# Two-matmul products for 256-token layers: joined activation parts in one 512-column stream, 256-column weight groups, feed-forward in quarters

## The chip, the cores and the metric

The kernel runs on one NeuronCore of a Trainium2 chip, as one program launched once. The metric is the device time of one execution in microseconds (us); lower is better. Three executions of the kernel before are known, and one more execution was profiled. The core's engines are named as the profile names them: PE (TensorE), with PEld for its weight loads, DVE (VectorE), ACT (ScalarE), POOL (GpSimd) and SP (SyncE, which here only starts transfers).

## The reference

The reference is a network in float32 on 256 tokens of width 2048, with 256 context tokens and 256 memory tokens. Two layers of a first block come first (projection `w_in`, attention with pooling and Fourier branches, gate, projection `w_out`; the context tokens go through layer 0 whole and give only keys and values in layer 1). Then a second block: an even layer (sparse attention and a recurrent mixer, `even_w_out`), an odd layer (a state-space mixer with `odd_w_in`, `s5_w_glu` and `odd_w_out`), and after each of the two an attention on the memory (`xattn_wq`, `xattn_wo`) and a feed-forward layer:

```python
h = rms_norm(x, g)                       # x: 256 tokens of 2048 channels
x = x + square(relu(h @ ffn_up)) @ ffn_down   # 2048 -> 8192 -> 2048
```

Nearly all of the arithmetic is products of a [256 or 512, K] activation with a weight matrix. They must keep float32 accuracy, which the kernel reaches by splitting both operands in two parts.

## The kernel before, in words

**Products.** Activations are held transposed, channels on partitions and tokens along the free axis. `split` (L306) cuts a float32 tensor into an upper part `hi`, a cast to `float32r` on ACT (L308), and a lower part `lo`, the rest, on DVE (L309). `weights` (L317) brings a weight tile of two 128-row blocks by 512 columns (512 KB) from HBM through `raw` (L311) into a buffer `wraw`, a DMA that SP starts (L314), and splits it into `wh` and `wl`. The activations lie in tiles `hl[:, k]` of shape [128, 2, 256]: for channel block k the upper part `xh` and, right behind it, the lower part `xl`.

`mm_t` (L336) makes out^T = W^T x. For every channel block k and every output tile j of 128 columns of W it issues three matmuls into the same 256 columns of a PSUM bank, `wh` by `xh` (L344), `wh` by `xl` (L345) and `wl` by `xh` (L346); below, such a k and j are called a pair. Each matmul has its own load of 128 by 128 weights. Two output tiles share a bank [128, 2, 256]. `mm_n` (L348) is the form with tokens on the output's partitions, with the weights as the 512-column stream.

`dense_t` (L354) walks over W in groups of 512 columns; each group takes two PSUM banks of the four that bear the name `acc`, runs over all channel blocks, and hands each bank to an `evac` function. It yields after every weight tile. Work in the background (generators in `self.bg`) is advanced by `tick` (L239) at a rate per yield. `dense_norm` (L476) is `dense_t` on an activation that is scaled and split at its first use (`scaled`, L464, and `scale_split`, L452, L455 on ACT and L456 on DVE). `add_evac` (L485) adds a bank to the residual stream with one DVE instruction of 128x512 (L491) and, where asked, adds squares to the next norm's sums (`stat_add`, L414 and L419).

**Buffers.** In the second block `wraw` has three buffers (`WR2`), `wh` and `wl` two (`WB2`) and, inside `wide`, a third. In the first block all have three.

**Feed-forward.** `ffn` (L1611) works in eight parts of 1024 hidden channels: `up(q)` fills a tile `hid` of eight blocks (two buffers of it), `down(q)` adds its product to the stream. The order is up 0, up 1, down 0, up 2, down 1, and so on. The evacuation of `up` squares the rectified values and splits them (L1626 to L1629, per bank). During the feed-forward of the even layer, `s5_gen` runs in the background; it prepares the odd layer's matrices, mostly on DVE.

**Order of the instructions.** Each engine has its own stream. The framework orders instructions within it by a simulated timeline and by the priority that follows from program order (`schedule_with_timeline_sim=True`); there is no order written out by hand for the products.

**Where products of 256 tokens are.** In layer 1 of the first block the gates (L876, columns 2560 on of `w_in`) and `w_out` (L920); in the even layer `rkv_gen` for one half of the heads (L1132), and `even_w_out` in two halves; `xattn_wq` and `xattn_wo`, twice each; `ffn_up` and `ffn_down`, twice each; `odd_w_in`, `s5_w_glu` and `odd_w_out`. Layer 0 of the first block has 512 tokens, so its `mm_t` streams 512 columns per matmul.

Of the kernel before, what the change touches and what calls it, by code (L numbers as in the profile page):

```python
# [14 lines left out]
ALU = mybir.AluOpType  # L15
# [31 lines left out]
# ---------------------------------------------------------------- host layouts  # L47
# [28 lines left out]
# channels of the state space layer: (32 groups) (4 of their 8 x 4: last) (8: first) (16 in a group)  # L76
# [35 lines left out]
# ---------------------------------------------------------------- constants of the shapes  # L112
# [29 lines left out]
def _make_consts1():  # L142
    # axial rope of 256 positions in rows of 64
# [44 lines left out]
def _pool_consts():  # L188
    """[n', group, n]: pooled[n] = sum over n' of u[n'] times this."""
# [11 lines left out]
def _dft_consts():  # L201
    cn, sn = _dft(256)
    a = np.stack([cn, sn], 1).astype(np.float32)  # [n', 2, n]
# [3 lines left out]
def _dftc_consts():  # L207
    cc, sc = _dft(128)
    nrm = 1.0 / np.sqrt(256.0 * 128.0)
    return np.stack([cc * nrm, -sc * nrm], 1).astype(np.float32)  # [c', 2, c]  # L210


# ---------------------------------------------------------------- the program
class Prog:
# [17 lines left out]
    def wide(self, name):  # L232
        """a third buffer for the parts of weights."""
# [4 lines left out]
    # ---- work in the background: generators that are advanced between steps of the foreground  # L238
# [62 lines left out]
    def held(self, op):  # L301
        """keeps an instruction behind those that its engine was given before, where that is asked for."""
# [14 lines left out]
    def weights(self, W, r0, nk, c0, ncols):  # L317
        """nk*128 rows of W from r0, ncols columns from c0, as an exact sum of two parts."""
        nc = self.nc
        w = self.raw(W, r0, nk, c0, ncols)  # L320
        self.turn = (self.turn + 1) % 3
        p, n = (self.wx, 1) if self.wx and self.turn == 0 else (self.wp, self.wbuf)
        wh = p.tile([128, KB, 512], F32R, name="wh", bufs=n)
        wl = p.tile([128, KB, 512], F32R, name="wl", bufs=n)
# [3 lines left out]
    def weights_in(self, p, tag, W, r0, c0):  # L328
        """the same for KB * 128 rows and 512 columns in memory of p."""
# [24 lines left out]
    def dense_t(self, W, r0, nk, c0, ncols, X, ntok, evac, mt=128, cstep=512):  # L354
        """out^T = W^T x: X(k) gives (hi, lo) as [128, ntok]; evac(first tile, bank [128, n, ntok])."""
        per = 512 // ntok
        for cb in range(0, ncols, cstep):
# [3 lines left out]
            for k0 in range(0, nk, KB):  # L361
                n = min(KB, nk - k0)
                wh, wl = self.weights(W, r0 + k0 * 128, n, c0 + cb, cw)
                for kk in range(n):
                    k = k0 + kk
                    xh, xl = X(k)
                    self.mm_t(accs, per, wh, wl, kk, cw, mt, xh, xl, k == 0, k == nk - 1)
# [8 lines left out]

    def dense_n(self, W, r0, nk, c0, ncols, X, tbs, evac, bank=None, pre=()):
        """out = x W in natural layout: X(k) gives (hi, lo) as [128, tokens]; evac(col offset, tb, bank [128, cols]).
        pre: memory (pool, tag) for the first steps' weights."""
        pre = list(pre)  # L380
        for cb in range(0, ncols, 512):
            cw = min(512, ncols - cb)
            accs = {tb: (bank or self.acc)() for tb in tbs}
            for k0 in range(0, nk, KB):
                n = min(KB, nk - k0)
                wh, wl = self.weights_in(*pre.pop(0), W, r0 + k0 * 128, c0 + cb) if pre else self.weights(W, r0 + k0 * 128, n, c0 + cb, cw)
                for kk in range(n):
                    k = k0 + kk
                    xh, xl = X(k)
                    for tb in tbs:  # L390
                        s = slice(tb * 128, tb * 128 + 128)
                        self.mm_n(accs[tb][:, :cw], wh, wl, kk, cw, xh[:, s], xl[:, s], k == 0, k == nk - 1)
# [28 lines left out]
    def stat_cols(self, st, out, pair):  # L421
        """PSUM columns out [128, 2 or 4]: the sums of every token block."""
# [10 lines left out]
    def bcast(self, cols, n):  # L433
        """columns [128 tokens, n] of token blocks as rows on all partitions: PSUM [128, n*128]."""
# [6 lines left out]
    def rstd_bc(self, st, eps, pair=True):  # L441
        """1/sqrt(mean square + eps) of every token, on all partitions, as a PSUM bank."""
# [9 lines left out]
    def scale_split(self, hl, src, g, p):  # L452
        """split of src [128, 256] times a column."""
# [4 lines left out]
    def rstd_tile(self, st, eps, p):  # L458
        """rstd_bc of a pair in SBUF."""
# [4 lines left out]
    def scaled(self, x, g, p):  # L464
        """X(k) of x * g, made at the first use."""
# [3 lines left out]
        def X(k):  # L469
# [3 lines left out]
            return hl[:, k, 0], hl[:, k, 1]  # L473
        return X

    def dense_norm(self, W, ncols, x, st, g, p, evac, rate=0.0):  # L476
        """out^T = W^T (x * g) for x [128, 16, 256], in columns of 512; evac(first tile, bank, 1/rms tile)."""
        X = self.scaled(x, g, p)
        r = []
        gen = self.dense_t(W, 0, KT, 0, ncols, X, T, lambda j, ps: evac(j, ps, r[0]))  # L480
# [1667 lines left out]
```

## Time and profile before

| | |
|---|---|
| three executions | 3907.92, 3908.26, 3910.87 us; median 3908.26 |
| the profiled execution, span | 3909.9 us |
| its instructions | 66146 |
| PE busy | 3725.4 us, 26960 matmuls |
| DVE busy | 2584.0 us |
| ACT busy | 1626.1 us |
| DMA | 701.46 MB, 179 GB/s on the mean |

The profiled execution's own time is known as its span, 3909.9 us from the first to the last instruction; it lies between the lowest and the highest of the three executions and 1.6 us above their median. PE is busy in nine tenths or more of nearly every fortieth of the span. A matmul's row in the profile covers its whole passage through the engine, and several are under way at once, so that the duration of one matmul (283 ns) is longer than the time from one start to the next. What a matmul costs is read from the distance of the starts. The granted clock of PE (PEclk) is 1.00 when it runs at 2.4 GHz and 0.5 at 1.2 GHz.

### The profile page before, as it was taken

Reading aid. Unit: us, or ns where it says so; the run is one execution under the profiler, and the core shown is the slowest. Engines: PE = TensorE matmul, PEld = TensorE weight load, DVE = VectorE, ACT = ScalarE, POOL = GpSimd, SP = SyncE. Lnnn points to the kernel's source line nnn. Section 1 sums busy time; section 2 is a strip of 40 time slices with the busy share of each in tenths; the row PEclk is TensorE's granted clock in tenths of the full one; section 3 lists DMA queues with packets and bytes.
Section 4 is the critical chain, followed back from the end, with each engine's and each line's share of the span. In section 5 each row is a group of like instructions: output and inputs, shape, how many; then the busy total and the mean of one; then the engine's idle time right before and its main releaser. Section 6 shows DMA issues by size and latency. Waiting matters only on the chain.

```text
span 3909.9 us, 66146 instructions
## 1 busy us (share of the span) xinstructions
PE 3725.4 (95%) x26960; PEld 3373.3 (86%) x26960; DVE 2584.0 (66%) x4288; ACT 1626.1 (42%) x2334; POOL 101.7 (3%) x138
## 2 busy tenths in 40 slices
PE   6999999999999999899999999999789999999998
PEld 2677777777899899788999999998679999999997
DVE  3578787666766878667967866675555665555555
ACT  3323233252454556335444433443334454444443
POOL 0010000001000001000000000000000000000000
PEclk8999999999999999999999999999889999999999
DMA  9645444555644434524656765668995455555554
GB/s 338 242 147 177 156 156 162 176 170 183 211 151 157 135 118 145 158 82 142 199 185 191 225 189 182 197 210 237 212 195 183 151 173 184 184 183 183 184 183 142
DMA packets 418913, 701.46 MB, mean 179 GB/s; under 512 B 52208, under 2 KB 112752, under 8 KB 415280
## 3 DMA queue, kind: packets, MB, share of 16 engines
q1 hardware_dynamic: 385840, 662.39, 55.0%
q10 hardware_dynamic: 31488, 30.64, 2.4%
q8 instruction: 211, 3.46, 0.4%
q0 software_dynamic: 1280, 4.20, 0.3%
q14 instruction: 94, 0.77, 0.1%
HBM read 672.63 MB, written 24.51 MB: 178 GB/s over the span
## 4 chain that ended last, share of the span: by engine, by line
PE 84%; DMA 8%; DVE 5%; ACT 2%; issue 1%; SPq 1%; ACTq 0%; POOL 0%; DVEq 0%; POOLq 0%
PE acc L344 21%; PE acc L346 21%; PE acc L345 21%; PE acc L350 3%; PE acc L352 3%; PE acc L351 3%; DMA wraw<-ada_w 2%; DVE wl L309 1%; PE sm L588 1%; DMA tts<-KD 1%; PE sm L565 1%; ACT wh L308 1%; DMA wraw<-w_in 1%; DMA xc<-xc 1%; PE sm L539 1%
## 5 line engine op out<-in xcount | busy, mean ns | idle before, releaser
L309 DVE TENSOR_TENSOR wl<-wraw,wh 128x1024 fp32r<-128x1024 f32 x994 | 1207.7, 1216 | 838.8 <-ACT wh L308 831.0
L308 ACT CAST wh<-wraw 128x1024 fp32r<-128x1024 f32 x994 | 1036.4, 1044 | 1663.4 <-PE acc L345 1241.8
L344 PE MATMUL acc<-hl,wh 128*128 128x256 f32 (+1 forms) x3696 | 1111.4, 303 | 17.4 <-ACT hl L455 7.3
L345 PE MATMUL acc<-hl,wh 128*128 128x256 f32 (+1 forms) x3696 | 1106.5, 301 | 3.1 <-DVE hl L456 3.1
L346 PE MATMUL acc<-hl,wl 128*128 128x256 f32 (+2 forms) x3696 | 1090.7, 301 | 4.8 <-DVE wl L309 4.8
L344 PEld LDWEIGHTS acc<-hl,wh 128*128 128x128 f32 x3696 | 704.7, 191 | 56.9 <-issue 15.7
L345 PEld LDWEIGHTS acc<-hl,wh 128*128 128x128 f32 x3696 | 706.2, 191 | 33.9 <-issue 10.3
L346 PEld LDWEIGHTS acc<-hl,wl 128*128 128x128 f32 (+1 forms) x3696 | 699.9, 192 | 38.4 <-issue 10.1
L344 PE MATMUL acc<-hid,wh 128*128 128x256 f32 x2048 | 577.6, 283 | 1.2 <-ACT wh L308 1.2
L345 PE MATMUL acc<-hid,wh 128*128 128x256 f32 x2048 | 577.1, 283 | 0.0
L346 PE MATMUL acc<-hid,wl 128*128 128x256 f32 x2048 | 574.5, 283 | 0.0
L344 PEld LDWEIGHTS acc<-hid,wh 128*128 128x128 f32 x2048 | 388.8, 190 | 1.8 <-ACT wh L308 1.4
L346 PEld LDWEIGHTS acc<-hid,wl 128*128 128x128 f32 x2048 | 387.9, 190 | 2.8 <-issue 2.6
L345 PEld LDWEIGHTS acc<-hid,wh 128*128 128x128 f32 x2048 | 389.4, 190 | 0.2 <-issue 0.2
L536 DVE SCALAR_TENSOR_TENSOR ada_a<-wraw,sc,ada_a 128x512 f32<-128x512 f32 x360 | 252.5, 745 | 17.2 <-DMA wraw<-ada_w 16.9
L350 PE MATMUL acc<-wh,hl 128*128 128x512 f32 (+1 forms) x504 | 200.0, 402 | 1.5 <-ACT hn_q L606 1.5
L351 PE MATMUL acc<-wh,hl 128*128 128x512 f32 (+1 forms) x504 | 199.8, 396 | 0.0
L352 PE MATMUL acc<-wl,hl 128*128 128x512 f32 (+1 forms) x504 | 188.6, 394 | 3.3 <-DVE wl L309 3.3
L350 PEld LDWEIGHTS acc<-wh,hl 128*128 128x128 f32 x504 | 96.6, 192 | 28.9 <-issue 4.0
L352 PEld LDWEIGHTS acc<-wl,hl 128*128 128x128 f32 x504 | 94.8, 190 | 27.8 <-DVE wl L309 5.6
L491 DVE TENSOR_TENSOR xc<-acc,xc 128x512 f32<-128x512 f32 x160 | 108.7, 689 | 9.9 <-PE acc L346 8.2
L351 PEld LDWEIGHTS acc<-wh,hl 128*128 128x128 f32 x504 | 96.3, 191 | 20.6 <-issue 2.0
(591 smaller groups left out, 4935.2 us busy)
## 6 DMA issues: line engine op xcount, KB each, us to landing
wraw<-ffn_up SPq DMA_DIRECT2D x256, 512.0 KB, 3.7
wraw<-ffn_down SPq DMA_DIRECT2D x256, 512.0 KB, 3.8
wraw<-ada_w SPq DMA_DIRECT2D x192, 512.0 KB, 4.5
wraw<-w_in SPq DMA_DIRECT2D x144, 512.0 KB, 4.4
wraw<-w_out SPq DMA_DIRECT2D x64, 512.0 KB, 4.7
wraw<-even_w_in SPq DMA_DIRECT2D x54, 512.0 KB, 3.6
wraw<-even_w_out SPq DMA_DIRECT2D x32, 512.0 KB, 3.6
wraw<-xattn_wkv SPq DMA_DIRECT2D x32, 512.0 KB, 4.7
```

The costliest lines, as they stand in the source:

```text
L308: nc.scalar.copy(hi, src)
L309: self.held(nc.vector.tensor_tensor(lo, src, hi.bitcast(F32), op=ALU.subtract))
L344: nc.tensor.matmul(A, h, xh, start=(start and first), stop=False)
L345: nc.tensor.matmul(A, h, xl, start=False, stop=False)
L346: nc.tensor.matmul(A, lo, xh, start=False, stop=(stop and last))
L350: nc.tensor.matmul(A, xh, wh[:, kk, :cw], start=start, stop=False)
L351: nc.tensor.matmul(A, xl, wh[:, kk, :cw], start=False, stop=False)
L352: nc.tensor.matmul(A, xh, wl[:, kk, :cw], start=False, stop=stop)
L491: nc.vector.tensor_tensor(x[:, j:j + n], ps, x[:, j:j + n], op=ALU.add)
L536: nc.vector.scalar_tensor_tensor(a[:, r], w[:, kk], c, a[:, r], op0=ALU.mult, op1=ALU.add)
L539: nc.tensor.matmul(acc[32 * cb:32 * cb + 32], self.cst("pick")[:, r], a[:, r], start=r == 0, stop=r == nr - 1)
L565: nc.tensor.matmul(S[:, off:off + w], qT[:, qb * 128:qb * 128 + 128], kT, start=i == 0, stop=i == len(kTs) - 1)
```

## The change

A new function `dense_p` takes the place of `dense_t` wherever the product has 256 tokens, but for the low-rank products of the recurrent mixer (`lora_gen`), the first half of `s5_w_glu` (`glu_gen`), `memkv` and `rkv_stream`, which stay as they were. Per pair it issues two matmuls: `wh` by the activation tile [128, 2, 256] as one stream of 512 columns into a whole PSUM bank, and `wl` by `xh` into the second half of that bank. The first half of the bank then holds `wh xh`, the second `wh xl + wl xh`, and the evacuation adds the halves.

A weight tile is now four 128-row blocks by 256 columns (also 512 KB, with rows of 1 KB instead of 2 KB in HBM). A group is 256 columns wide and takes two banks, one for each output tile. `add_evac`, the new `out_evac_p` of layer 1 and the odd layer's `out_evac` add each half of each bank to the stream with its own DVE instruction. All other evacuations go through `joined`: a copy of one half by ACT and an addition by DVE for each bank, into an SBUF tile [128, 2, 256], which the old evacuation then reads.

The feed-forward works in four parts of 2048 hidden channels with one `hid` tile of sixteen blocks: up 0, down 0, up 1, down 1, and so on. Comments and docstrings are dropped throughout, and `X(k)` returns the joined tile. The core of the diff:

```diff
-    def raw(self, W, r0, nk, c0, ncols, tag="wraw"):
+    def raw(self, W, r0, nk, c0, ncols, tag="wraw", kb=KB):
...
-        w = p.tile([128, KB, 512], F32, name="wraw", tag=tag, bufs=bufs)
+        w = p.tile([128, kb, KB * 512 // kb], F32, name="wraw", tag=tag, bufs=bufs)
...
+    def dense_p(self, W, r0, nk, c0, ncols, X, evac):
+        nc = self.nc
+        kb = 2 * KB
+        for cb in range(0, ncols, 256):
+            accs = [self.acc((2, T)) for _ in range(2)]
+            for k0 in range(0, nk, kb):
+                wh, wl = self.weights(W, r0 + k0 * 128, kb, c0 + cb, 256, kb)
+                for kk in range(kb):
+                    k = k0 + kk
+                    xp = X(k)
+                    for j, A in enumerate(accs):
+                        cs = slice(128 * j, 128 * j + 128)
+                        nc.tensor.matmul(A, wh[:, kk, cs], xp, start=k == 0, stop=False)
+                        nc.tensor.matmul(A[:, 1], wl[:, kk, cs], xp[:, 0], start=False, stop=k == nk - 1)
+                    if kk == 1 and self.sub:
+                        self.tick(self.sub)
+                if k0 + kb < nk:
+                    yield
+            evac(cb // 128, accs)
+            yield
+
+    def joined(self, f, p, bufs=1):
+        def evac(j, accs):
+            s = p.tile([128, 2, T], F32, name="joined", bufs=bufs)
+            for i, A in enumerate(accs):
+                self.nc.scalar.copy(s[:, i], A[:, 1])
+                self.nc.vector.tensor_tensor(s[:, i], A[:, 0], s[:, i], op=ALU.add)
+            f(j, s)
+        return evac
...
-        def f(j, ps):
-            n = ps.shape[1]
-            nc.vector.tensor_tensor(x[:, j:j + n], ps, x[:, j:j + n], op=ALU.add)
+        def f(j, accs):
+            for h in range(2):
+                for i, A in enumerate(accs):
+                    nc.vector.tensor_tensor(x[:, j + i], A[:, h], x[:, j + i], op=ALU.add)
...
-                        yield from self.dense_t(W, 0, KT, 2560 + c0, 512, Xt, nt, gate_evac(c0))
+                        if last:
+                            yield from self.dense_p(W, 0, KT, 2560 + c0, 512, Xt, self.joined(gate_evac(c0), p))
+                        else:
+                            yield from self.dense_t(W, 0, KT, 2560 + c0, 512, Xt, nt, gate_evac(c0))
...
-                    n = 15 - turns(gt, K1)
+                    n = (11 if last and g else 15) - turns(gt, K1)
...
-        HT, NQ = 8, 8
+        HT, NQ = 16, 4
...
-            def up(q):
-                hid[q] = p.tile([128, HT, 2, T], F32R, name="hid", bufs=2)
+            for q in range(NQ):
+                hid = p.tile([128, HT, 2, T], F32R, name="hid")
...
-                gen = self.dense_t(a["ffn_up_2"][l], 0, KT, q * HT * 128, HT * 128, X, T, evac)
+                gen = self.dense_p(a["ffn_up_2"][l], 0, KT, q * HT * 128, HT * 128, X, self.joined(evac, p))
...
-            up(0)
-            for q in range(1, NQ):
-                up(q)
-                down(q - 1)
-            down(NQ - 1)
+                self.run(self.dense_p(a["ffn_down_2"][l], q * HT * 128, HT, 0, D, lambda k: hid[:, k], self.add_evac(x, st_out if q == NQ - 1 else None)), rate)
```

## Rows read from the trace of the kernel before

**Rows 1.** The page: busy time of PE, then the shares of the last chain.

```profile
PE 3725.4 (95%) x26960; PEld 3373.3 (86%) x26960; DVE 2584.0 (66%) x4288; ACT 1626.1 (42%) x2334; POOL 101.7 (3%) x138
...
PE 84%; DMA 8%; DVE 5%; ACT 2%; issue 1%; SPq 1%; ACTq 0%; POOL 0%; DVEq 0%; POOLq 0%
```

**Rows 2.** Windows: busy us (count) of each engine, PEclk, DMA share, GB/s.

```profile
1500.00:1600.00 100.00, 96.02 (x837) 90.96 (x836) 85.16 (x174) 56.47 (x112) 12.41 (x18) 1.00 0.49 156
1838.00:1862.00 24.00, 21.75 (x169) 21.34 (x168) 21.72 (x56) 14.73 (x26) 3.06 (x3) 0.93 0.51 160
2640.00:2700.00 60.00, 55.07 (x455) 52.06 (x455) 34.61 (x58) 22.83 (x31) 0.87 (x1) 0.94 0.81 239
3200.00:3800.00 600.00, 600.00 (x5002) 600.00 (x5002) 338.63 (x343) 250.24 (x266) 0.00 (x0) 1.00 0.59 183
```

**Rows 3.** Timeline of the second feed-forward layer: start us, us, matmuls 48 apart.

```profile
3400.21 0.28 PE L344 MATMUL acc<-hl,wh 128*128 128x256 f32 x1
...
3405.97 0.28 PE L344 MATMUL acc<-hl,wh 128*128 128x256 f32 x1
```

**Rows 4.** Timeline of PE in layer 0's `w_out`: matmuls 51 apart.

```profile
640.05 0.39 PE L344 MATMUL acc<-hl,wh 128*128 128x512 f32 x1
...
651.61 0.39 PE L344 MATMUL acc<-hl,wh 128*128 128x512 f32 x1
```

**Rows 5.** Groups by line and form: the first of every pair's three matmuls.

```profile
L344 PE MATMUL acc<-hl,wh 128*128 128x256 f32 x3168 | 902.4, 287 | 11.7 <-ACT hl L455 7.3 <-ACT wh L308 4.1 <-DVE rope_t L691 0.2
L344 PE MATMUL acc<-hid,wh 128*128 128x256 f32 x2048 | 577.6, 283 | 1.2 <-ACT wh L308 1.2
...
L344 PE MATMUL acc<-mx,wh 128*128 128x256 f32 x256 | 72.4, 286 | 3.4 <-ACT mx L308 3.4
...
L344 PE MATMUL acc<-yh,wh 128*128 128x256 f32 x256 | 71.1, 283 | 0.0
...
L344 PE MATMUL acc<-yb,wh 128*128 128x256 f32 x128 | 36.4, 294 | 0.0
L344 PE MATMUL acc<-ya,wh 128*128 128x256 f32 x128 | 36.0, 286 | 0.1
...
L344 PE MATMUL acc<-xol,wh 128*128 128x256 f32 x128 | 33.7, 287 | 0.0
```

**Rows 6.** Groups by line and form: the split of a weight tile.

```profile
L309 DVE TENSOR_TENSOR wl<-wraw,wh 128x1024 fp32r<-128x1024 f32 x976 | 1192.4, 1223 | 829.0 <-ACT wh L308 821.5 <-PE acc L346 3.5 <-PE sm L751 1.6
L308 ACT CAST wh<-wraw 128x1024 fp32r<-128x1024 f32 x976 | 1022.9, 1049 | 1644.8 <-PE acc L345 1233.8 <-PE acc L351 130.0 <-DMA wraw<-w_in 47.4
```

**Rows 7.** Waits from 3200 to 3800: us in total, times, longest.

```profile
ACT wh L308 <- PE acc L345: 326.6, 195, 1.8
```

**Rows 8.** DMA: weight loads issued from 3200 to 3800, 512 KB each.

```profile
DMA to landing us min/median/max: 3.4/3.7/5.1
```

**Rows 9.** DMA queues from 0 to 40: packets, MB, share of 16 engines.

```profile
q10 hardware_dynamic: 5866, 7.08, 51.5%
q1 hardware_dynamic: 3592, 6.93, 48.6%
```

**Rows 10.** DMA issues with rows of 1152 bytes: KB each, us to landing.

```profile
wraw<-even_w_in SPq DMA_DIRECT2D x8, 288.0 KB, 2.9
```

**Rows 11.** Groups by line and form: evacuations and their like, DVE and ACT.

```profile
L491 DVE TENSOR_TENSOR xc<-acc,xc 128x512 f32<-128x512 f32 x160 | 108.7, 689 | 9.9 <-PE acc L346 8.2
...
L419 DVE TENSOR_TENSOR sqacc<-sqacc,sqt 128x512 f32<-128x512 f32 x93 | 63.4, 686 | 41.6 <-ACT sqt L414 38.4
...
L1626 ACT ACTIVATE ff_r<-acc 128x512 f32<-128x512 f32 x64 | 38.0, 596 | 40.7 <-PE acc L346 40.7
...
L787 DVE TENSOR_TENSOR nt<-xc,bc 128x256 f32<-128x256 f32 x64 | 24.8, 420 | 8.6 <-ACT bc L779 8.1
...
L584 ACT COPY att_PT<-sm 128x256 f32<-128x256 f32 x48 | 16.4, 370 | 15.6 <-PE sm L583 15.0
```

**Rows 12.** Groups by line and form: the scaled activation's lower part.

```profile
L456 DVE SCALAR_TENSOR_TENSOR hl<-xc,cols,hl 128x256 fp32r<-128x256 f32 x80 | 33.3, 475 | 1.2 <-ACT hl L455 1.2
```

More of the change, by code (lines that the diff above doesn't have):

```diff
@@ L479, in dense_norm @@
         r = []
-        gen = self.dense_t(W, 0, KT, 0, ncols, X, T, lambda j, ps: evac(j, ps, r[0]))
+        gen = self.dense_p(W, 0, KT, 0, ncols, X, self.joined(lambda j, ps: evac(j, ps, r[0]), p))
         self.step(gen, 2, rate)
@@ L906, in out_evac, with out_evac_p @@
             def out_evac(j, ps):
-                n = ps.shape[1]
-                if not last:
-                    x0 = op.tile([128, 2, T], F32, name="x0", bufs=4)
-                    nc.gpsimd.dma_start(x0, a["xc0"][:, j * 128:j * 128 + 128].rearrange("r p t -> p r t"))
-                for i in range(n):
-                    for r in range(nt // T):
-                        xs = xc[:, r, j + i]
-                        nc.vector.scalar_tensor_tensor(xs, ps[:, i, r * T:r * T + T], adac[:, r, 32 + j + i:33 + j + i], xs if last else x0[:, r], op0=ALU.mult, op1=ALU.add)
-                if last:
-                    for s in st_out:
-                        self.stat_add(s, xc[:, 0, j:j + 2], self.col("final_norm_g")[:, j:j + 2] if s is st_out[1] else None)
-                else:
-                    self.stat_add(st_out, xc[:, :, j])
-            self.run(self.dense_t(WO, 0, KT, 0, D, lambda k: (mx[:, k, 0, :nt], mx[:, k, 1, :nt]), nt, out_evac), RATE)
+                x0 = op.tile([128, 2, T], F32, name="x0", bufs=4)
+                nc.gpsimd.dma_start(x0, a["xc0"][:, j * 128:j * 128 + 128].rearrange("r p t -> p r t"))
+                for r in range(2):
+                    nc.vector.scalar_tensor_tensor(xc[:, r, j], ps[:, 0, r * T:r * T + T], adac[:, r, 32 + j:33 + j], x0[:, r], op0=ALU.mult, op1=ALU.add)
+                self.stat_add(st_out, xc[:, :, j])
+            def out_evac_p(j, accs):
+                for h in range(2):
+                    for i, A in enumerate(accs):
+                        xs = xc[:, 0, j + i]
+                        nc.vector.scalar_tensor_tensor(xs, A[:, h], adac[:, 0, 32 + j + i:33 + j + i], xs, op0=ALU.mult, op1=ALU.add)
+                for s in st_out:
+                    self.stat_add(s, xc[:, 0, j:j + 2], self.col("final_norm_g")[:, j:j + 2] if s is st_out[1] else None)
+            Xm = lambda k: mx[:, k, :, :nt]
+            self.run(self.dense_p(WO, 0, KT, 0, D, Xm, out_evac_p) if last else self.dense_t(WO, 0, KT, 0, D, Xm, nt, out_evac), RATE)
             self.flush()
@@ L949, in dsa @@
         W = a["even_w_in_2"][0]
-        X = lambda k: (hl[:, k, 0], hl[:, k, 1])
+        X = lambda k: hl[:, k]
         id_ = self.cst("ident")
@@ L1138, in evac @@
                 self.shift_mix(ps, bc, mu, lambda i: t[:, j + i], p)
-            yield from self.dense_t(self.a["even_w_in_2"][0], 0, KT, 880 + c0 + 512 * g, 512, lambda k: (hl[:, k, 0], hl[:, k, 1]), T, evac)
+            yield from self.dense_p(self.a["even_w_in_2"][0], 0, KT, 880 + c0 + 512 * g, 512, lambda k: hl[:, k], self.joined(evac, p))
     def rkv_stream(self, x, bc, g, rT, kT, vT, p, q):
@@ L1525, in even @@
                 self.split(yb[:, j, 0], yb[:, j, 1], xc[:, 0, 8 + j])
-            self.run(self.dense_t(WO, 1024, 8, 0, D, lambda k: (yb[:, k, 0], yb[:, k, 1]), T, self.add_evac(x, st_out)))
+            self.run(self.dense_p(WO, 1024, 8, 0, D, lambda k: yb[:, k], self.add_evac(x, st_out)))
     def middle_stats(self, st, f):
@@ L1636, in up @@
                 self.run(gen, rate)
-            def down(q):
-                self.run(self.dense_t(a["ffn_down_2"][l], q * HT * 128, HT, 0, D, lambda k: (hid[q][:, k, 0], hid[q][:, k, 1]), T,
-                                      self.add_evac(x, st_out if q == NQ - 1 else None)), rate)
-            up(0)
-            for q in range(1, NQ):
-                up(q)
-                down(q - 1)
-            down(NQ - 1)
+                self.run(self.dense_p(a["ffn_down_2"][l], q * HT * 128, HT, 0, D, lambda k: hid[:, k], self.add_evac(x, st_out if q == NQ - 1 else None)), rate)
             self.flush()
@@ L1994, in odd, with out_evac @@
                     glu_evac(4 * cb + 2 * i, accs[cb][i])
-            self.run(self.dense_t(a["s5_w_glu"], 0, KT, 1024, 1024, lambda k: (zh[:, k, 0], zh[:, k, 1]), T, lambda j, ps: glu_evac(8 + j, ps)))
-            def out_evac(j, ps):
-                n = ps.shape[1]
-                for i in range(n):
-                    xv = x[:, j + i].rearrange("p (c t) -> p t c", t=8)
-                    nc.vector.tensor_tensor(xv, ps[:, i].rearrange("p (t c) -> p t c", t=8), xv, op=ALU.add)
-                self.stat_add(st_out, x[:, j:j + n])
-            self.run(self.dense_t(a["odd_w_out"], 0, KT, 0, D, lambda k: (yh[:, k, 0], yh[:, k, 1]), T, out_evac))
+            self.run(self.dense_p(a["s5_w_glu"], 0, KT, 1024, 1024, lambda k: zh[:, k], self.joined(lambda j, ps: glu_evac(8 + j, ps), p)))
+            def out_evac(j, accs):
+                for h in range(2):
+                    for i, A in enumerate(accs):
+                        xv = x[:, j + i].rearrange("p (c t) -> p t c", t=8)
+                        nc.vector.tensor_tensor(xv, A[:, h].rearrange("p (t c) -> p t c", t=8), xv, op=ALU.add)
+                self.stat_add(st_out, x[:, j:j + 2])
+            self.run(self.dense_p(a["odd_w_out"], 0, KT, 0, D, lambda k: yh[:, k], out_evac))
     def build(self):
```

50 lines of the change are left out of this document (24 added, 26 removed).

## The prediction

> **What bounds the kernel now.** I read the page first: PE is busy 95% of the span and makes up 84% of the chain that ended last [rows 1]. A mean can hide stages with other limits, so I cut the span into windows next. In the second feed-forward layer (3200 to 3800) PE never pauses, at the full clock, while DVE is busy 56%, ACT 42% and the DMA engines 59% [rows 2]. Other windows are less clean: from 1500 to 1600 DVE is busy 85%, and around the odd layer's first product the DMA share is 0.81 and PE has 5 us of holes in 60 [rows 2]. But products dominate, so the price of a product is the distance between the starts of its matmuls. The timeline gives it at two widths. At 256 columns, 48 matmuls take 5.76 us, 120.0 ns each [rows 3]. At 512 columns, 51 matmuls take 11.56 us, 226.7 ns each [rows 4]. The reader should see that the difference, 106.7 ns, is 256 columns at 2.4 GHz, and that 13.3 ns stay per matmul whatever its width. Each matmul's load of 128 weight columns is hidden at both widths.
>
> **Matmuls.** A pair costs 3 x 120.0 = 360.0 ns now. After, one wide and one narrow matmul: 226.7 + 120.0 = 346.7 ns. The streamed columns are the same 768; what goes is one matmul's fixed 13.3 ns. That this holds for widths that alternate is an estimate from rows of unmixed widths: the loads have the same 128 columns in both, and 256 streamed columns hide one already.
>
> The pairs: the first matmul of a pair has 3168 + 2048 + 256 + 256 + 3 x 128 = 6112 instructions at 256 columns in the tiles that the change concerns [rows 5]. Of the 3168, 32 in `lora_gen` (two whole tiles by 16 blocks) and 128 in `glu_gen` (8 by 16) stay, so 5952 pairs are converted, 4096 of them in the feed-forward. 5952 x 13.33 ns = **79.4 us** less of PE time.
>
> Here a rule speaks against the gain. The Trainium skill, "TensorE: Matmul & The Clock Gate", section "Back-to-back issue gap", gives the distance of two isolated matmuls at full clock as columns/2.4 plus 2.5 ns. By that rule a removed matmul is worth 2.5 ns and the change 5952 x 2.5 = 15 us, an estimate. The trace does not agree: its constant is 13.3 ns.
>
> **Weight split.** 5952/8 = 744 weight tiles still need 1.05 us of ACT and 1.22 us of DVE each [rows 6], unchanged. PE takes 8 x 346.7 = 2.77 us per tile instead of 2.88, so DVE's share of the split rises from 42% to 44%. In the window ACT's cast waited for PE to free `wh` 195 times in 209 tiles, 326.6 us in all [rows 7]: over 1.6 us of slack per tile against 0.11 us lost. Nothing.
>
> **DMA.** The same bytes come in rows of 1 KB instead of 2 KB. First the landing: with three raw buffers a load may take 3 x 2.77 - 1.05 - 1.22 = 6.0 us; it takes 3.7 (5.1 at most) now [rows 8]. Then the packets. In the feed-forward one 2 KB packet costs 105 ns of a DMA engine (0.59 x 16 engines over 183 GB/s). From 0 to 40 us, when the engines are full, the queue of 2 KB weight rows spends 0.486 x 640 us / 3592 = 87 ns per packet of 1.93 KB, and the queue with mostly 1 KB rows 0.515 x 640 / 5866 = 56 ns per packet of 1.21 KB [rows 9]: 45 and 46 ns per KB. So a 1 KB packet costs between 46 ns and, if size didn't matter, 105 ns. I take 53, half a 2 KB packet: 32 packets per engine and tile, 1.7 us of the 2.77. Rows cut from a wider matrix, as here, land well too: 256 rows of 1152 bytes in 2.9 us [rows 10], so 256 more packets could add 2.9 us at the very most, and by their bytes they add nothing. SP issues the same number of DMAs. I take zero.
>
> **Evacuations.** `add_evac` did one 128x512 addition per two output tiles, 0.689 us; now four of 128x256 at 0.42 each [rows 11], 1.68 us. `ffn_down` does it for four parts instead of eight, so its DVE time stays (8 x 0.689 = 5.5 against 4 x 1.68 = 6.7 us per two tiles), behind an 11.1 us group. It is not hidden in `xattn_wo`, which has four channel blocks only, one weight tile per group: DVE needs 1.22 + 1.68 + 0.69 (squares, [rows 11]) = 3.59 us per group, PE 2.77. Sixteen groups x 0.82 = 13 us; the first tiles are split ahead of time, so I take **10**, between 0 and 13.
>
> `joined` adds per two tiles two ACT copies of 0.37 and two DVE additions of 0.42. In `ffn_up` DVE then has 4 x 1.22 + 0.84 + 3 x 0.69 = 7.8 us in an 11.1 us group, hidden. In the even layer, `even_w_out`'s first half (8 x 1.68 - 8 x 0.689 = 8 us) and `rkv_gen` (12 x 0.42 = 5 us) add 13 us to a DVE that is 85% busy [rows 2]; they lie behind the chunk work. Between 0 and 13, I take **3**.
>
> **Starts of a product.** In five products the activation is scaled as it is used. A channel block lasted four pairs, 1.44 us; now two, 0.69 us, while DVE needs 0.475 [rows 12] + 1.22/4 = 0.78 us. 0.09 x 16 blocks x 5 = **7 us**. PE's mean clock there is already down to 0.93 [rows 2], which at the lower level gives DVE time; I keep 7 for both, with 0 and 20 as ends.
>
> **Feed-forward order.** `down(q)` follows `up(q)` at once. The last two blocks of `hid` are wanted 14 x 0.693 = 9.7 us after `up` ends; the chain to them is a copy 0.37, two additions 0.84, relu 0.60, two products 1.38, cast about 0.6 and rest 0.69, some 4.5 us [rows 11], plus up to two weight splits in between. Hidden, as long as it stays under 9.7; nothing for eight handovers, 40 us if the whole chain showed.
>
> **What PE cannot use.** Layer 1's gates and `odd_w_in` (512 pairs, 6.8 us of the gain) run beside DMA-bound work [rows 2]; I take **4** as lost, between 0 and 6.8.
>
> **Sum.** 79.4 - 10 - 3 - 7 - 4 = 55 us off the profiled span of 3909.9 us, which stands 1.6 us above the median 3908.3. So 3908.3 - 55 = **3853 us**. With the ends: 79 us off is 3829; 13 + 13 + 20 + 7 = 53 given back leaves 26 off, 3882.
>
> **Rivals.** First, *the handovers show*: the chain from `up` to `hid` is queued behind weight splits and `s5_gen`'s DVE work, and each of the eight handovers costs 5 us. With the middle terms, 24 + 40 = 64 us are given back and 15 stay: 3893. For it: one `hid` and one `joined` buffer, and a chain through both engines. Against: 5 us of margin and DVE at 56% [rows 2].
>
> Second, *the DMA becomes the bound*, the case on the slower side. Its place is every converted tile; it decides once a 1 KB packet costs more than 2.88 us / 32 = 90 ns. At the 2 KB packet's 105 ns a tile takes 3.38 us, and 744 x 0.50 = 372 us are added: 4280. At 92 ns it is 744 x 0.064 = 48 us, 3956. For it: no row of this trace has strided 1 KB rows alone. Against: 46 ns per KB when the engines are full [rows 9].
>
> Third, *the removed matmul is free*: a wide matmul between narrow ones takes twice 120 ns, not 226.7. Then nothing is gained and the middle terms remain: 3908 + 24 = 3932, or 3908 if they vanish. Against: both widths show the same 13.3 ns [rows 3, 4]. The skill's rule above lies near this case; by its 15 us the time would be 3917, an estimate.
>
> **Chances.** Forecast 0.77, handovers 0.11, DMA 0.06, free matmul 0.06. The range takes the forecast's ends and the first rival: 3829 to 3893; it leaves out 0.12 of rivals and a little of the forecast. A measurement of this kernel tells 0.2% (8 us) from no change. Faster: 0.77 + 0.11 = 0.88. The third rival is half within 8 us and half slower: the same 0.03, slower 0.06 + 0.03 = 0.09.
>
> **What would show it.** Right: in the second feed-forward, starts in the order 512, 256 columns, 227 and 120 ns apart; 744 tiles of 2.77 us; 21008 matmuls; DMA share near 0.6; ACT's cast still waits for PE. The `xattn_wo` stretch shows PE waiting for DVE. Wrong: a pair at other than 347 ns, casts waiting for the DMA, landings over 6 us, or PE idle at the start of each `down`.

## The result, and the profile after

| | before | after | ratio (95%) |
|---|---|---|---|
| median us | 3909.57 | 3849.62 | 0.9844 (0.9830 to 0.9857) |
| lowest to highest, 4 runs each | 3907.92 to 3913.00 | 3847.68 to 3850.04 | |

The change takes 60 us off. The forecast was 3853, its range 3829 to 3893. The total came out right; two of its terms did not, and that their errors cancelled is luck. The experiments below show which.

The page of the changed kernel, busy times and the chain that ended last, against [rows 1]:

```profile
span 3848.3 us, 54892 instructions
...
PE 3654.7 (95%) x21008; PEld 3029.0 (79%) x21008; DVE 2694.8 (70%) x4732; ACT 1680.5 (44%) x2524; POOL 102.1 (3%) x138
...
PE 82%; DMA 9%; DVE 6%; ACT 2%; issue 1%; SPq 0%; ACTq 0%; POOL 0%; DVEq 0%; POOLq 0%
```

PE has the 5952 matmuls fewer and is busy 70.7 us less, not 79.4. It is still the bound. The window of the second feed-forward layer, with the columns of [rows 2]:

```profile
3155.00:3755.00 600.00, 600.00 (x3444) 523.41 (x3443) 373.89 (x461) 272.35 (x333) 0.00 (x0) 1.00 0.62 188
```

PE still never pauses, at the full clock; DVE went from 56% to 62%, the DMA share from 0.59 to 0.62. The timeline of PE there, in a lower product (start us, us, then the matmul), against [rows 3, 4]:

```profile
3400.64 0.39 PE L392 MATMUL acc<-hid,wh 128*128 128x512 f32 x1
3400.87 0.27 PE L393 MATMUL acc<-hid,wl 128*128 128x256 f32 x1
3400.99 0.40 PE L392 MATMUL acc<-hid,wh 128*128 128x512 f32 x1
...
3405.84 0.40 PE L392 MATMUL acc<-hid,wh 128*128 128x512 f32 x1
```

Wide and narrow alternate, 230 and 120 ns apart as far as the 10 ns of a row tell. From the first to the last row are 15 pairs in 5.20 us: 346.7 ns a pair, as forecast. But not everywhere. The same view of an upper product of the same layer:

```profile
3331.66 0.40 PE L392 MATMUL acc<-hl,wh 128*128 128x512 f32 x1
...
3340.14 0.40 PE L392 MATMUL acc<-hl,wh 128*128 128x512 f32 x1
```

These are 24 pairs in 8.48 us, 353.3 ns each, with no pause between any two matmuls. In the upper products such stretches last some 11 us and alternate with as long ones of 346.7, and nothing like them is in the profile before. Added up over the starts of successive matmuls, from the layer's first to its last lower product, the excess over 226.7 and 120.0 ns is 3.0 us. The first feed-forward layer has a third length:

```profile
2217.90 0.39 PE L392 MATMUL acc<-hid,wh 128*128 128x512 f32 x1
...
2223.15 0.39 PE L392 MATMUL acc<-hid,wh 128*128 128x512 f32 x1
```

These are 15 pairs in 5.25 us, 350.0 ns each, and nearly all pairs of that layer are so. Over the 1583 of them that follow each other undisturbed the excess is 5.5 us.

DMA queue and issues of the second feed-forward layer's window, and the waits of ACT's cast and of DVE's addition, against [rows 7 to 9]:

```profile
q1 hardware_dynamic: 113220, 112.44, 61.2%
...
wraw<-ffn_up SPq DMA_DIRECT2D x108, 512.0 KB, 3.7
wraw<-ffn_down SPq DMA_DIRECT2D x107, 512.0 KB, 3.7
```

```profile
ACT wh L308 <- PE acc L392: 217.1, 129, 4.1
...
DVE xc L526 <- PE acc L393: 14.5, 22, 2.5
```

A packet of 1 KB takes 0.612 x 16 x 600 us / 113220 = 51.9 ns, and a tile lands in 3.7 us, as before. The cast still waits for PE and never for the DMA.

**Where the time went.** I read the starts of the first and last matmul of each product from the timelines of five profiles: the two kernels, each profiled twice, and the first experiment, in which only the merging is undone. A row is the time from one such point to the next; "gain" is 13.3 ns for each converted pair of the row.

| stage, us | gain | before | again | three narrow | after | again |
|---|---|---|---|---|---|---|
| start to layer 1's `w_out` | 3.4 | 1122.1 | 1121.6 | 1125.0 | 1126.4 | 1127.1 |
| `w_out` | 3.4 | 94.3 | 94.3 | 94.4 | 91.7 | 92.4 |
| even layer, to `xattn_wo` | 6.8 | 597.5 | 593.1 | 604.6 | 592.3 | 590.9 |
| `xattn_wo` | 0.9 | 27.2 | 27.2 | 27.9 | 26.9 | 27.0 |
| to the first lower product | 3.4 | 97.7 | 97.7 | 97.2 | 97.5 | 96.6 |
| first feed-forward, to its last lower product | 23.9 | 697.6 | 699.9 | 685.4 | 668.5 | 668.4 |
| odd layer, to `odd_w_out` | 5.1 | 350.5 | 348.1 | 341.9 | 341.9 | 345.8 |
| `odd_w_out` | 3.4 | 93.1 | 92.6 | 93.8 | 92.9 | 92.7 |
| to the second `xattn_wo` | 0.9 | 39.1 | 39.4 | 38.2 | 40.3 | 40.1 |
| second `xattn_wo` | 0.9 | 27.2 | 27.2 | 27.8 | 27.1 | 26.9 |
| to the first lower product | 3.4 | 96.3 | 96.3 | 98.5 | 96.2 | 96.3 |
| second feed-forward | 23.9 | 645.0 | 645.0 | 645.0 | 624.0 | 624.1 |

The two feed-forward layers hold 50 of the 60 us. Each kernel repeats itself within 0.1 to 2.3 us there. The odd layer does not (3.9 us between two profiles of one kernel), so nothing is read from it, and the even layer moves by 1.4 and 4.5 us.

### The profile page after: what moved, and what is told of

Its sections match the earlier page's. It is cut to its first block, busy times and chain, and to the rows that moved or that the text cites. A ratio compares the mean times of both kernels' runs of the same rounds, so it can differ in the third digit from the quotient of the medians.

```text
span 3848.3 us, 54892 instructions
## 1 busy us (share of the span) xinstructions
PE 3654.7 (95%) x21008; PEld 3029.0 (79%) x21008; DVE 2694.8 (70%) x4732; ACT 1680.5 (44%) x2524; POOL 102.1 (3%) x138
## 4 chain that ended last, share of the span: by engine, by line
PE 82%; DMA 9%; DVE 6%; ACT 2%; issue 1%; SPq 0%; ACTq 0%; POOL 0%; DVEq 0%; POOLq 0%
PE acc L392 33%; PE acc L393 17%; PE acc L344 4%; PE acc L345 4%; PE acc L346 4%; PE acc L350 3%; PE acc L352 3%; PE acc L351 3%; DMA wraw<-ada_w 2%; DVE wl L309 2%; PE sm L623 1%; ACT wh L308 1%; PE sm L600 1%; DMA wraw<-w_in 1%; DMA tts<-KD 1%
## 5 line engine op out<-in xcount | busy, mean ns | idle before, releaser
L392 PE MATMUL acc<-hl,wh 128*128 128x512 f32 x3008 | 1060.4, 400 | 21.9 <-DVE hl L490 15.1
L393 PE MATMUL acc<-hl,wl 128*128 128x256 f32 x3008 | 827.3, 284 | 4.3 <-DVE wl L309 4.3
L392 PE MATMUL acc<-hid,wh 128*128 128x512 f32 x2048 | 709.9, 394 | 1.4 <-DVE xc L526 1.0
L392 PEld LDWEIGHTS acc<-hl,wh 128*128 128x128 f32 x3008 | 559.3, 190 | 150.4 <-DVE hl L490 11.6
L393 PEld LDWEIGHTS acc<-hl,wl 128*128 128x128 f32 x3008 | 567.9, 190 | 23.4 <-DVE wl L309 8.1
L392 PEld LDWEIGHTS acc<-hid,wh 128*128 128x128 f32 x2048 | 378.3, 188 | 85.6 <-issue 1.8
L344 PE MATMUL acc<-hl,wh 128*128 128x512 f32 (+2 forms) x688 | 256.0, 376 | 7.7 <-ACT wh L308 3.8
L345 PE MATMUL acc<-hl,wh 128*128 128x512 f32 (+2 forms) x688 | 252.9, 369 | 0.0
L346 PE MATMUL acc<-hl,wl 128*128 128x512 f32 (+2 forms) x688 | 247.1, 369 | 0.0
L344 PEld LDWEIGHTS acc<-hl,wh 128*128 128x128 f32 (+1 forms) x688 | 130.2, 190 | 37.3 <-issue 6.6
L345 PEld LDWEIGHTS acc<-hl,wh 128*128 128x128 f32 (+1 forms) x688 | 130.0, 189 | 25.2 <-issue 5.9
L346 PEld LDWEIGHTS acc<-hl,wl 128*128 128x128 f32 (+1 forms) x688 | 129.1, 189 | 23.9 <-issue 3.2
```

The lines of the kernel that those rows point to most:

```text
L344: nc.tensor.matmul(A, h, xh, start=(start and first), stop=False)
L345: nc.tensor.matmul(A, h, xl, start=False, stop=False)
L346: nc.tensor.matmul(A, lo, xh, start=False, stop=(stop and last))
L392: nc.tensor.matmul(A, wh[:, kk, cs], xp, start=k == 0, stop=False)
L393: nc.tensor.matmul(A[:, 1], wl[:, kk, cs], xp[:, 0], start=False, stop=k == nk - 1)
```

## The experiments

The medians of the timed ones, each against runs of the kernel before on the same chip. The kernel before had a median of 3906.24 us beside experiments 1, 2, 4 and 5 and of 3904.59 beside 3 and 8, where the result has 3909.57. So a difference between a median here and the 3849.6 of the result is uncertain by some 5 us for this alone.

| kernel | median us | ratio (95%) |
|---|---|---|
| three narrow matmuls everywhere | 3904.64 | 0.9998 (0.9986 to 1.0009) |
| feed-forward alone changed | 3854.47 | 0.9865 (0.9851 to 0.9880) |
| upper products in three narrow matmuls | 3871.40 | 0.9916 (0.9900 to 0.9933) |
| feed-forward in eighths | 3846.60 | 0.9847 (0.9829 to 0.9864) |
| `xattn_wo` as before | 3849.14 | 0.9854 (0.9839 to 0.9868) |
| wide, wide, narrow, narrow | 3853.11 | 0.9865 (0.9844 to 0.9887) |
| the same in eighths | 3853.45 | 0.9870 (0.9849 to 0.9891) |

**1. Only the merging undone.**

```diff
-                        nc.tensor.matmul(A, wh[:, kk, cs], xp, start=k == 0, stop=False)
+                        nc.tensor.matmul(A[:, 0], wh[:, kk, cs], xp[:, 0], start=k == 0, stop=False)
+                        nc.tensor.matmul(A[:, 1], wh[:, kk, cs], xp[:, 1], start=False, stop=False)
```

> Only the merging is undone: the tile shape, the 256-column groups, the joining and the feed-forward in quarters stay, but each wide matmul is two of 256 columns again. Theory (each of the 5952 removed matmuls took 13.3 ns beyond its columns): 3849.6 + 79 = 3929 us, between 3915 and 3940, and so some 20 us above the kernel before, which is what the rest of the change costs. By the rival that the removed matmul was free and the time came from the new order and the new tiles: 3840 to 3860. The Trainium skill's 2.5 ns for each matmul would give 3865. If the theory holds, pairs of this kernel take 360.0 ns in the trace.

Neither number came: 3904.6. The gain is the merging's, since without it nothing is left of it, but it is 55.0 us by the medians (9.2 ns a pair), 60 by the two ratios (10.1 ns), and not 79. The Trainium skill's 2.5 ns for an isolated matmul ("TensorE: Matmul & The Clock Gate", "Back-to-back issue gap") does not agree either: by it this kernel would have stood at 3865, an estimate. And the rest of the change costs nothing in sum, not 20 us. The timeline of its second feed-forward layer shows the pairs at 360.0 ns, four in 1.44 us:

```profile
3434.45 0.28 PE L392 MATMUL acc<-hid,wh 128*128 128x256 f32 x1
3434.57 0.28 PE L393 MATMUL acc<-hid,wh 128*128 128x256 f32 x1
3434.69 0.28 PE L394 MATMUL acc<-hid,wl 128*128 128x256 f32 x1
3434.81 0.28 PE L392 MATMUL acc<-hid,wh 128*128 128x256 f32 x1
...
3435.89 0.28 PE L392 MATMUL acc<-hid,wh 128*128 128x256 f32 x1
```

There is no stretch of any other length in that layer, whose excess is below 0.2 us in both upper and lower products. By the stage table the rest of the change costs 10 us up to the first `xattn_wo` (in this one profile) and saves 12 us in the first feed-forward layer, before any matmul is merged. In the second layer, of the same products, it saves nothing. What the first has and the second lacks is the state-space preparation, whose 256 small matmuls lie between the products'. The groups by line and form in that stage, of the kernel before and of this one (busy, mean | idle before):

```profile
L1805 PE MATMUL sm<-H,bd 128*32 128x128 f32 x256 | 29.5, 281 | 0.0
```

```profile
L1834 PE MATMUL sm<-H,bd 128*32 128x128 f32 x256 | 20.5, 280 | 0.0
```

They stand in 63 separate places of the timeline before and in 39 here. From the start of each to the start of what follows it, with the delay ahead of the first, they take 34.6 us before and 23.1 here: 11.5 of the 12.2 us. Counted in the same way, the changed kernel has 36 places and 22.2 us, and experiment 4 has 32 and 19.2: fewer places, less time. That the shorter column groups place them so is argued from the orders, not tried by itself.

**2. The feed-forward alone changed** (the kernel before, with the new product and quarters in these layers only).

```diff
-            self.run(self.dense_t(...))
+            self.run(self.dense_p(...))
```

> The kernel before with the feed-forward layers alone changed (4096 of the 5952 pairs); all other products are as before. From the two traces the layers gained 29 and 21 us: theory 3909.6 - 50 = 3860 us, between 3853 and 3866, so that the other products together are worth some 10 us of the 60, less than the 24.7 that their 1856 pairs come to at 13.3 ns. Rival: the other products gave nothing or lost, and this kernel is as fast as the changed one or faster: 3845 to 3851.

3854.5, at the lower end of the theory's range: a gain of 51.8 us over the 3906.24 beside it. The other products, whose 1856 pairs come to 24.7 us at 13.3 ns, are worth about 5 us, within what the intervals can tell from nothing. Its two feed-forward stages take 668.5 and 624.1 us, exactly those of the changed kernel, and its odd layer 347.4.

**3. Three narrow matmuls in the upper products alone.**

```diff
-                gen = self.dense_p(a["ffn_up_2"][l], ..., self.joined(evac, p))
+                gen = self.dense_p(a["ffn_up_2"][l], ..., self.joined(evac, p), False)
```

> The changed kernel with three 256-column matmuls again in the upper products of the feed-forward layers alone (2048 pairs). If each removed matmul is worth its 13.3 ns everywhere: 3849.6 + 27.3 = 3877. If the stretches of 353.3 ns, which lie mostly in the upper products, take a third of that gain there and go with it: 3849.6 + 18 = 3868, and the lower products show 346.7 ns throughout. From three narrow matmuls everywhere (3904.6), the 5952 pairs averaged 9.2 ns: 3868 as well.

3871.4 lies between the two, and an interval of some 13 us does not part them. The steadier second layer does: 632.2 us instead of 624.0. That is 8.2 us for the 768 upper pairs of this stage, which come to 10.2 at 13.3 ns. The stretches are gone from the upper products (excess below 0.2 us); in the lower ones 0.9 us is left, at the head of each.

**4. Feed-forward in eighths,** an upper product issued ahead of each lower one.

```diff
-        HT, NQ = 16, 4
+        HT, NQ = 8, 8
...
+            up(0)
+            for q in range(1, NQ):
+                up(q)
+                down(q - 1)
+            down(NQ - 1)
```

> The changed kernel with the feed-forward layers again in eighths, an upper product issued ahead of each lower one and two buffers for the hidden part. It doubles the additions into the stream (256 more column groups' worth of DVE work for both layers, some 50 us of DVE in each). Theory (the handovers of the quarters cost nothing, and DVE has room): within 5 us of 3849.6. Rival (each of the handovers hides a stop of some 2 us of PE): about 12 us faster, 3838. Second rival (the doubled additions hold up the splitting of weights on DVE): over 10 us slower.

3846.6, 3 us lower, and well inside its interval: the handovers cost nothing that shows, and the doubled additions (in both layers together 64 column groups and 256 additions more, where the text says 256 groups) are hidden as well. The stages take 664.6 and 624.9 us.

**5. `xattn_wo` as before.**

```diff
-            self.run(self.dense_p(a["xattn_wo_2"][l], 0, 4, 0, D, lambda k: ol[:, k], self.add_evac(x, st_out)))
+            self.run(self.dense_t(a["xattn_wo_2"][l], 0, 4, 0, D, lambda k: ol[:, k], T, self.add_evac_t(x, st_out)))
```

> The changed kernel with the output product of the memory attention in both layers as before (512-column groups, three matmuls, one addition for a bank). By the prediction's term the new form costs 10 us there beyond its matmuls' gain of 3.4 us (256 pairs at 13.3 ns), so that this kernel would be some 7 us faster: 3843. By the trace of the changed kernel, PE waits there for the additions only some 3 us in a layer: between 2 us faster and 3 us slower than 3849.6.

3849.1: nothing comes back in the total. Both `xattn_wo` take 27.2 us in this kernel, against 26.9 and 27.1 in the new form. All that PE waits for the additions there, by the waits of PE in the changed kernel around the first one (total, times, longest):

```profile
PE acc L392 <- DVE xc L526: 0.9, 3, 0.5
```

But the total hides two differences that cancel. From `xattn_wo` to the first lower product this kernel takes 94.4 us in the first layer and 95.3 in the second, the changed kernel 97.5 and 96.2 (96.6 and 96.3 in its second profile). So 3 to 4 us do come back behind the product, although 1.7 us that its pairs had gained are given up (they are 128, where the text says 256). Against that, the second feed-forward layer takes 629.9 instead of 624.1 us, since its lower products run at 353.3 ns a pair. Experiment 9 shows what decides that.

**6. Rows of 512 bytes,** two transfers for a tile.

```diff
-        self.nc.sync.dma_start(w[:, :nk, :ncols], W[...])
+        h = 128 if kb > KB else ncols
+        for o in range(0, ncols, h):
+            self.nc.sync.dma_start(w[:, :nk, o:o + h], W[..., c0 + o:c0 + o + h])
```

> The changed kernel with each weight tile of the new form loaded by two transfers of 128 columns (rows of 512 B), so twice the packets for the same bytes. In the second feed-forward layer a 1 KB packet takes 51.9 ns of one of 16 DMA engines and the queue is busy 61.2%. Theory (a packet's time goes with its bytes, as from 2 KB to 1 KB): 26 ns each, the same share, within 8 us of 3849.6. Rival (a packet of 512 B takes as long as one of 1 KB): the queue would need 122% of the layer's time, so that the layers become bound by DMA: 22% of some 1600 us, 350 us slower, 4200.

One run took 3853.0. DMA queue and issues of its second feed-forward layer, 3155 to 3755:

```profile
q1 hardware_dynamic: 227016, 112.74, 64.4%
...
wraw<-ffn_up SPq DMA_DIRECT2D x218, 256.0 KB, 3.2
wraw<-ffn_down SPq DMA_DIRECT2D x210, 256.0 KB, 3.1
```

Twice the packets, 0.644 x 16 x 600 / 227016 = 27.2 ns each. From 105 [rows 2] over 51.9 to 27.2 ns, the price goes with the bytes. The rival that the DMA becomes the bound is off by far.

**7. Both kernels once more,** unedited.

> The kernel before, profiled a second time. Between the profile of before and that of three narrow matmuls everywhere, two stages differ that hold few changed products or none that got shorter: the first feed-forward layer from its first to its last lower product (697.6 against 685.4 us) and from there to the last product of the odd layer (350.6 against 341.9). If these 20.9 us come from the new form (its shorter column groups place the small matmuls of the state-space preparation otherwise), this profile shows 697 and 350 again, within 3. If they are scatter from execution to execution, at least one of the two moves by 5 us or more.

> The changed kernel, profiled a second time: the same two stages took 668.5 and 341.9 us. Within 3 us of these if the stages are steady; 5 us or more away if they scatter. The stretches of 353.3 ns come back in the upper products of the second feed-forward layer if they belong to the program.

One run each: 3906.6 and 3852.7. Their stages stand in the table. The first feed-forward layer is the program's (697.6 and 699.9; 668.5 and 668.4), with the small matmuls at 29.5 us busy again. The odd layer scatters (348.1; 345.8 where 341.9 was): its 8.6 us between before and after are not shown to be the change's. The stretches of 353.3 ns came back at the same tiles of the upper products.

**8. Another order: wide, wide, narrow, narrow,** alone and in eighths.

```diff
                     for j, A in enumerate(accs):
-                        nc.tensor.matmul(A, wh[:, kk, cs], xp, ...)
-                        nc.tensor.matmul(A[:, 1], wl[:, kk, cs], xp[:, 0], ...)
+                        nc.tensor.matmul(A, wh[:, kk, 128 * j:128 * j + 128], xp, ...)
+                    for j, A in enumerate(accs):
+                        nc.tensor.matmul(A[:, 1], wl[:, kk, 128 * j:128 * j + 128], xp[:, 0], ...)
```

> The changed kernel with another order inside a step: the wide matmuls of both columns' halves first, then both narrow ones, where wide and narrow alternated. In the trace of the changed kernel the pairs of long stretches take 353.3 ns instead of 346.7, which sums to 3.0 us in seven eighths of the second feed-forward layer and 6.1 us in the first. Theory (the extra belongs to a narrow matmul that follows its own wide one): the stretches of 353.3 ns go, and the time falls by 7 to 12 us, to 3838 to 3843. Rival (it belongs to the wide matmul, or to what the other engines do at the time): the stretches stay and the time is within 4 us of 3849.6.

> Feed-forward in eighths with an upper product ahead of each lower one (3846.6 by itself) together with the order wide, wide, narrow, narrow. If the stretches of 353.3 ns go with the order: 3835 to 3841, the fastest so far. If they stay: 3843 to 3850.

3853.1 and 3853.5: no gain. In the first the second layer's stage takes the same 624.1 us, but with pairs of another length. The timeline of an upper product (x2: two in a row):

```profile
3330.03 0.63 PE L391 MATMUL acc<-hl,wh 128*128 128x512 f32 x2
3330.49 0.39 PE L393 MATMUL acc<-hl,wl 128*128 128x256 f32 x2
...
3343.26 0.63 PE L391 MATMUL acc<-hl,wh 128*128 128x512 f32 x2
```

From the first row to the last are 38 pairs in 13.23 us, 348.2 ns each, and so it is throughout the layer: no stretch of 353.3 ns is left, none of 346.7 either, and the excess is again 3.0 us. In the first layer the pairs take 352.0 ns on the mean, and its stage 676.6 us instead of 668.5. So the order does set the length of a pair, but a narrow matmul behind its own wide one is not what costs: that theory's gain falls.

**9. What sets off the stretches:** the squared relu on POOL, then left out, in the second layer.

```diff
-                    nc.vector.tensor_tensor(s, s, ...)
-                    nc.vector.tensor_tensor(v, v, s, op=ALU.mult)
+                    eng = nc.gpsimd if l else nc.vector
+                    eng.tensor_tensor(s, s, ...)
+                    eng.tensor_tensor(v, v, s, op=ALU.mult)
```

```diff
-                    v = p.tile([128, 2, T], F32, name="ff_r")
+                    if l == 0:
+                        v = p.tile([128, 2, T], F32, name="ff_r")
...
+                    else:
+                        v = s
```

> The changed kernel with the two products of the squared relu in the second feed-forward layer on POOL instead of DVE. The stretches of 353.3 ns a pair begin and end there with these two instructions (in the group looked at they ran from 3306.7 to 3308.1 us and the stretch began at 3307.8). If they set them off, the stretches of the second layer move, shrink or go (3.6 us at most, so the time between the first and the last lower product falls from 624.0 to 621 to 623 us); if not, the pattern and 624.0 stay.

> The changed kernel with the relu and the two products of its square left out in the second feed-forward layer (the hidden part is then the joined product itself; the output is another). If the stretches of 353.3 ns come from these instructions, they are gone: 621 us between the first and the last lower product. If they come from the additions that join the banks, from the split or from the wide matmuls alone, they stay in some place: 623 to 624.5 us.

One run each, 3848.8 and 3851.7. Left out, the relu takes nothing with it: 623.7 us, and the stretches stay at the same tiles of the upper products. On POOL they grew: 626.9 us, because in two of the four quarters almost the whole lower product runs at the longer pair. The timeline of one of them:

```profile
3419.95 0.40 PE L392 MATMUL acc<-hid,wh 128*128 128x512 f32 x1
3420.30 0.40 PE L392 MATMUL acc<-hid,wh 128*128 128x512 f32 x1
...
3429.84 0.40 PE L392 MATMUL acc<-hid,wh 128*128 128x512 f32 x1
```

From the first row to the last are 28 pairs in 9.89 us, 353.2 ns each, where the changed kernel has 346.7 (3400.64 to 3405.84 above). So these instructions aren't the cause. What the changes of length go with is the order of the matmuls in PE's own stream. The rows of the changed kernel just ahead of the stretch of 353.3 ns shown with the result:

```profile
3329.44 0.27 PE L393 MATMUL acc<-hl,wl 128*128 128x256 f32 x1
3329.55 0.62 PE L392 MATMUL acc<-hl,wh 128*128 128x512 f32 x2
3330.01 0.40 PE L393 MATMUL acc<-hl,wl 128*128 128x256 f32 x2
3330.25 0.40 PE L392 MATMUL acc<-hl,wh 128*128 128x512 f32 x1
```

Wide and narrow alternate, but here two wide and then two narrow matmuls follow each other. Between the first and the last lower product of the second layer are 41 places with two wide in a row and then, at once or a few pairs on, two narrow. The length changes at every one of them, from 346.7 to 353.3 ns or back, and nowhere else; a lower product runs through seven column groups without such a place and keeps its length. The same holds for the second layer in both kernels of this experiment and in that of experiment 5. Which length a lower product gets is then a matter of how many such places lie ahead of it: in the changed kernel all four have the shorter one, on POOL two have the longer, and in experiment 5 all four. In the first layer such places leave the 350.1 ns as they are. This is read from the traces; no edit moved one such place alone.

## Why the prediction was right, and which of its steps were not

**The bound and the rivals.** Right: PE stays the bound at the full clock, and the merging is what gains (experiment 1). *The DMA becomes the bound*: wrong, a 1 KB packet takes 51.9 ns against the 90 that it needs, and even rows of 512 bytes do not do it (experiment 6). *The handovers show*: wrong by experiment 4 and by the groups by line of the changed kernel (busy, mean | idle before, releasers), where all lower products of both layers together wait 1.4 us:

```profile
L392 PE MATMUL acc<-hid,wh 128*128 128x512 f32 x2048 | 709.9, 394 | 1.4 <-DVE xc L526 1.0 <-ACT wh L308 0.4
```

*The removed matmul is free*: wrong, it is worth 9.2 to 10.1 ns on average, which is also what stands against the 2.5 ns of the Trainium skill's "TensorE: Matmul & The Clock Gate" ("Back-to-back issue gap").

**Matmuls, 79.4 us: mis-sized; experiment 1 measures 55.0 to 60.** The step that failed is "this holds for widths that alternate is an estimate from rows of unmixed widths". It holds in most lower products of the second layer. In the stretches of 353.3 ns a pair is worth 6.7 ns instead of 13.3, and in the first layer, at 350.1, 9.9: a pair at other than 347 ns, which the prediction named as a sign of being wrong. This takes 8.5 us (3.0 + 5.5) out of the 47.8 that the two large feed-forward stages should gain. The merged stages then gained 16.9 and 21.0 us. Outside these stages 31.6 us were to come and, from three narrow to after, 16 came. In `odd_w_out` PE halts some 0.2 us at the head of each column group and 0.9 of the 3.4 us came; ahead of `w_out` nothing came, as term 4 had it.

**`xattn_wo`, 10 us: too much, 4 to 5.** The step took DVE's 3.59 us for a group against PE's 2.77 and let all the difference show. But the stretch was never PE's: 64 pairs of 360 ns are 23.0 us, and it took 27.2 before. The excess of DVE's work overlaps in part with what PE waited for already and runs on into the next product, where it meets the wait below. Experiment 5 gets some 3 us back there, after giving up the 1.7 us of its pairs.

**Starts of a product, 7 us: the mechanism another, the size near.** PE does not fall behind block by block. It waits once, since the wide matmul wants both parts of block 0 (the pair of `hl` parts is its one stream). The waits of PE over the whole span, of the kernel after and of the one before:

```profile
PE acc L392 <- DVE hl L490: 15.1, 4, 4.4
```

```profile
PE acc L344 <- ACT hl L455: 7.3, 4, 2.7
PE acc L345 <- DVE hl L456: 3.1, 4, 1.0
```

15.1 against 10.4 us: 4.7 more in four starts. With three narrow matmuls in the new form it is 12.3, and in experiment 5 13.0, so part of it is the merging's and part the additions' of `xattn_wo`.

**Even layer, 3 us; gates and `odd_w_in`, 4 us.** From before to three narrow, the joining costs 7.1 us in the even layer (11.5 against the second profile of before); the merging then gains 12.3 there. The sum is near what was said, but the parts rest on one profile of three narrow, in a stage that takes from 589.2 to 596.1 us in kernels with the same code there (experiments 3, 4, 5 and 9), so they are not shown. Ahead of `w_out` 4.3 us were lost rather than 3.4 gained; but the kernel with the feed-forward alone changed reaches `w_out` at 1125.2 as well, so most of that isn't the gates'.

**Left out of the sum: the small matmuls of the first feed-forward layer, 12 us gained.** The prediction cost the products alone there and said nothing of what PE does between them.

So 79.4 - 24 = 55 was forecast, and 60 came: the merging gave 55.0 to 60, the rest of the change 0 to 8 (1.6 by the medians of experiment 1, 7.6 by the two profiles), its costs of some 10 to 15 us, in one profile, paid back in the first feed-forward layer. **DMA, weight split and feed-forward order, each 0**: right (51.9 ns for a packet where 53 was taken; landing 3.7 us; experiment 4).

No version beat the changed kernel by more than the intervals.

## What to carry to other kernels

A matmul has a fixed price besides its columns, so merging two streams that share a weight tile pays where PE never pauses, and little where it does: 51.8 of the 60 us came from the feed-forward layers, and the other products could be left as they were at about 5 us. Test a sum by undoing the one term that carries it; a total that fits can hide two errors of some 20 us each. Compare stages and not only totals: putting `xattn_wo` back seemed to change nothing, because a later stage lost what it gained. And look at the bounding engine's whole stream, at what else it does between the instructions that you count and in which order they stand.

## What the runs showed of the hardware that was not expected

The wide-and-narrow pair has more than one length at the same granted clock of 1.00 and without a wait: 346.7 and 353.3 ns in the second feed-forward layer, 350.1 in the first, and 348.3 in the second where two wide and two narrow follow each other throughout (experiment 8). In the second layer the length changes wherever the order slips once from wide, narrow to wide, wide, narrow, narrow, and then stays, for as long as 87 us on POOL (experiment 9). It comes back at the same tiles in every profile of a program. It is not seen in three narrow matmuls (experiments 1 and 3) and is not the squared relu's (9). What in PE holds the length, and why the first layer has another, stays open; the longer pairs cost this kernel some 9 us in the two large stages.
